# Pooling edges of two blocks as one product over gathered rows, another order in the mixer, and one side of a unit made at once

## The chip, the cores and the metric

The kernel runs on one core of a Trainium2 chip. A core has five engines that run side by side and wait for each other by semaphores: TensorE (PE, matrix products; PEld is its loading of the stationary operand), VectorE (DVE), ScalarE (ACT), GpSimd (POOL) and SyncE (SP), which here only issues transfers. Sixteen DMA engines move the data. The metric is the time of one execution on the device in microseconds (us).

## The reference

One sequence of 512 tokens with 1024 channels passes two layers, all in float32. Layer 0 mixes tokens by pooling, layer 1 by attention over a sliding window; behind each stands a feed-forward network (FFN). What matters here is layer 0's mixer and the first product of both FFNs:

```python
POOL_WINDOWS = (2, 4, 8, 16)          # one for each group of 256 channels
h = rms_norm(x, mix_pre_g[layer])
# per group: mean over the last w tokens (fewer at the start) minus the token itself
mean = (csum[:, 1:, sl] - csum[:, lo, sl]) / cnt[None, :, None]
diffs.append(mean - hf[..., sl])
m = einsum('bsgc,gcd->bsgd', d, w_pool).reshape(B, S, D) * scale
x = x + rms_norm(m, mix_post_g[layer])
u = rms_norm(x, ffn_pre_g[layer]) @ w_in     # 1024 -> 2 * 2816: gate and value
# then a causal convolution of width 3, gelu(gate) * value, and @ w_out
x = x + rms_norm(f, ffn_post_g[layer])
```

## The kernel before

**Blocks.** The tokens stand in four blocks of 128, a block with its tokens on the 128 partitions. The mixer goes through the blocks: the norm of the block (`mix_norm`, lines 379 to 394) leaves `xm`; the pooling (`mix_pool`, 403 to 418) multiplies `xm` with a band matrix and so also transposes it: for each chunk of 128 channels one product makes the block's own 128 output tokens. A window of up to 16 tokens reaches back into the block before, so for blocks 1 to 3 a second product for each chunk (line 416) adds, over the first 16 output tokens, what the previous block's rows give. Eight chunks a block, four to a PSUM bank (`pd`, a bank a half). ScalarE copies both banks to `d`. `mix_map` (420 to 427) multiplies `d` with the group weights `wp`, which VectorE has scaled beforehand (`mix_weights`, 396 to 401) with the channel gains and with `scale_row`, the row of scales spread over the partitions by a product with ones. `mix_post` (a norm, a gain, and the sum into `x`), `mix_pre` (the FFN's norm, `xn_f`) and `mix_T` (eight transposes by PE into `tr_f`) follow; ScalarE copies the transposes to `xTh`, the high part, and VectorE subtracts for `xTl`, the rest.

**Products in two parts.** The large products run as three passes of a faster format: high x high, high x rest, rest x high (`mm3`, 341 to 344). Weights come as `raw` from DRAM by a unit of 1 MB; ScalarE casts them to `wh`, VectorE makes `wl` (`piece`, 205 to 230, by a quarter; `split`, 232 to 262, by a half). `raw` has two buffers, `wh` and `wl` three. A unit of the first FFN product (`up`, 519 to 530) makes 128 gate channels (side 0) and 128 value channels (side 1): for each side eight chunks of the input, three passes each, into a PSUM bank. While not all blocks of `xT` are there, a unit is made for blocks 0 and 1 (256 columns) and later for 2 and 3; the rest of the units run over all 512 columns. The mixed products of the mixer itself are plain float32 and appear as two passes each.

**Order.** The order of PE, ACT, DVE and POOL is the order in which the program issues the instructions (lines 438 to 483 for the mixer, 1128 to 1136 for layer 1); each engine takes its own in that order and waits where an operand isn't ready. SP's transfers are put in order by the framework's scheduler, which holds one back where it isn't ready. SP starts with `x`, the band, constants, the pool weights (unit 0 of the list, `U_POOL`), the rows of gains and the first two units of the FFN (`u0`, `u1`; lines 349 to 362). `u1` takes the `raw` buffer of the pool weights. A block of filler products (`keep_busy`, 366 to 375) runs on PE while the first data come. PSUM has eight banks, all from one ring.

The lines of the mixer's order in the middle, where blocks overlap, are:

```python
    d2 = mix_pool(2)
    piece(u0, 0)
    mix_T(0)
    mix_pre(1)
    piece(u0, 1)
    acc2 = mix_map(2, d2)
```

Of the kernel before, what the change touches and what calls it, by code (L numbers as in the profile page):

```python
# [8 lines left out]
F32 = mybir.dt.float32  # L9
# [51 lines left out]
def _pieces(v, bits, n):  # L61
    out = []
    for _ in range(n - 1):
        q = 2.0 ** (math.floor(math.log2(v)) + 1 - bits)
        c = math.floor(v / q) * q
        out.append(c)
        v -= c
    out.append(float(np.float32(v)))
    return out


def build(nc, tc, ctx, a, out):
# [7 lines left out]
    def bank(name):  # L80
        return ps.tile([P, 512], F32, tag="ps", name=name)
# [193 lines left out]
    def square(junk, src, ss, h, first):  # L275

        nc.scalar.activation(junk, src, AF.Square, scale=1.0 / math.sqrt(D), accum_out=ss[:, h : h + 1])  # L277
        if first:
            nc.gpsimd.tensor_scalar(ss[:, h : h + 1], ss[:, h : h + 1], EPS, None, ALU.add)  # L279

    def new_ss(name):
        return pc.tile([P, 4], F32, tag="ss", name=f"ss_{name}", bufs=6)

    def rstd_end(ss):
        nc.gpsimd.tensor_tensor(ss[:, 2:3], ss[:, 0:1], ss[:, 1:2], ALU.add)
        nc.gpsimd.tensor_tensor(ss[:, 3:4], ss[:, 2:3], mhalf, ALU.pow)
        return ss[:, 3:4]
# [8 lines left out]
    def halves(t):  # L296
        return [t[:, h * 512 : (h + 1) * 512] for h in range(2)]

    def post_norm(b, acc, grow, name, pool=None):
        if pool is None:  # L300
            ts_ = halves(pc.tile([P, D], F32, tag="t4", name=f"pt_{name}{b}", bufs=3))
        else:
            ts_ = [pool.tile([P, 512], F32, tag="qT", name=f"pt_{name}{b}_{h}", bufs=2) for h in range(2)]
        r = rstd_of(acc, ts_, f"p_{name}{b}")
        gs, xs = halves(grow), halves(x[b])
        for h in range(2):
            nc.vector.tensor_tensor(ts_[h], acc[h], gs[h], ALU.mult)
        for h in range(2):
            nc.vector.scalar_tensor_tensor(xs[h], ts_[h], r, xs[h], ALU.mult, ALU.add)
# [45 lines left out]
    nc.sync.dma_start(x[2], a["x"][2])  # L355
    post_row = bcast_row(a["mix_post_g"][0], "mpost0")
    nc.sync.dma_start(x[3], a["x"][3])
    load(U_IN[0])
    pre_row = bcast_row(a["ffn_pre_g"][0], "fpre0")
    load(U_IN[0] + 1)  # L360
    nc.sync.dma_start(cst[:, C_LATE:C_FREQ], a["cst"][:, C_LATE:C_FREQ])
    load_conv(0)
    scale_row = [bank(f"scale_row{h}") for h in range(2)]
    scratch = bank("scratch")

    def keep_busy(n):

        for _ in range(n):
            nc.tensor.matmul(scratch[:, :P], warm, warm, start=True, stop=True)

    keep_busy(13)

    for h in range(2):
        nc.tensor.matmul(scale_row[h], warm, row[:, h * 512 : (h + 1) * 512], start=True, stop=True)
    keep_busy(1)
    wp = pm.tile([P, 8, 256], F32, tag="wp", name="wp")
    xns, xnf = {}, {}

    def mix_norm(b):
        xm = pm.tile([P, D], F32, tag="xm", name=f"xm{b}", bufs=NB)  # L380
        ss = new_ss(f"m{b}")
        xs, junk = halves(x[b]), halves(xm)
        if b < 2:

            nc.scalar.activation(junk[0], xs[0], AF.Square, scale=1.0 / math.sqrt(D), accum_out=ss[:, 0:1])
            nc.vector.tensor_tensor_reduce(out=junk[1], in0=xs[1], in1=xs[1], scale=1.0 / D, scalar=EPS,
                                           op0=ALU.mult, op1=ALU.add, accum_out=ss[:, 1:2])
        else:
            for h in range(2):
                square(junk[h], xs[h], ss, h, h == 0)  # L390
        r = rstd_end(ss)
        for h in range(2):
            nc.vector.tensor_scalar(halves(xm)[h], halves(x[b])[h], r, None, ALU.mult)
        xns[b] = xm

    def mix_weights():
        pr = raws[U_POOL]
        for c in range(8):
            g = c // 2
            nc.vector.scalar_tensor_tensor(wp[:, c, :], pr[:, c * 256 : (c + 1) * 256], gain_col(0, c),  # L400
                                           scale_row[g // 2][:, (g % 2) * 256 : (g % 2 + 1) * 256], ALU.mult, ALU.mult)

    def mix_pool(b):
        d = pm.tile([P, D], F32, tag="d", name=f"d{b}", bufs=2)
        for h in range(2):
            pd = bank(f"pd{b}{h}")
            for k in range(4):
                c = h * 4 + k
                g = c // 2
                cs = slice(c * P, (c + 1) * P)  # L410
                o = pd[:, k * P : (k + 1) * P]
                if b == 0:
                    nc.tensor.matmul(o, xns[b][:, cs], band[:, g, P + EDGE :], start=True, stop=True)
                else:
                    nc.tensor.matmul(o, xns[b][:, cs], band[:, g, :P], start=True, stop=False)
                    nc.tensor.matmul(o[:, :EDGE], xns[b - 1][:, cs], band[:, g, P : P + EDGE], start=False, stop=True)
            nc.scalar.copy(d[:, h * 512 : (h + 1) * 512], pd)
        return d

    def mix_map(b, d):  # L420
        acc = [bank(f"my{b}{h}") for h in range(2)]
        for g in range(4):
            o = acc[g // 2][:, (g % 2) * 256 : (g % 2) * 256 + 256]
            for k in range(2):
                c = g * 2 + k
                nc.tensor.matmul(o, d[:, c * P : (c + 1) * P], wp[:, c, :], start=k == 0, stop=k == 1)  # L426
        return acc

    def mix_post(b, acc):
        post_norm(b, acc, post_row, "m0")  # L430

    def mix_pre(b):
        xnf[b] = pre_norm(b, pre_row, "f0")

    def mix_T(b):
        transpose_in(b, xnf[b], xT, "f0")

    u0, u1 = U_IN[0], U_IN[0] + 1
    mix_norm(0)
    mix_norm(1)  # L440
    d0 = mix_pool(0)
    mix_weights()
    mix_norm(2)
    d1 = mix_pool(1)
    acc0 = mix_map(0, d0)
    mix_post(0, acc0)
    mix_norm(3)
    acc1 = mix_map(1, d1)
    mix_pre(0)
    mix_post(1, acc1)  # L450
    d2 = mix_pool(2)
    piece(u0, 0)
    mix_T(0)
    mix_pre(1)
    piece(u0, 1)
    acc2 = mix_map(2, d2)
    piece(u0, 2)
    mix_post(2, acc2)
    d3 = mix_pool(3)
    mix_T(1)  # L460
    piece(u0, 3)
    mix_pre(2)
    acc3 = mix_map(3, d3)
    piece(u1, 0, defer=True)
    piece(u1, 1, defer=True)
    mix_post(3, acc3)
    while deferred:
        deferred.pop(0)()
    piece(u1, 2)
    piece(u1, 3)  # L470
    mix_pre(3)

    def start0():
        yield 0, (0, 2)
        mix_T(2)
        yield 1, (0, 2), (0,)
        mix_T(3)
        ctx_mix.close()
        yield 1, (0, 2), (1,)
        ahead(U_IN[0])  # L480
        rope_tables()
        yield 0, (2, 4)
        yield 1, (2, 4)


    sin_t = pc.tile([P, NB, 32], F32, tag="sin", name="sin_t")
# [29 lines left out]
        nc.scalar.activation(cos_t, ang, AF.Sin)  # L516


    def up(l, xT, j, accs, blks, sides=(0, 1)):
        hi, lo = slots[U_IN[l] + j]  # L520
        hi4 = hi.rearrange("p (k s c) -> p k s c", k=KC, s=2)
        lo4 = lo.rearrange("p (k s c) -> p k s c", k=KC, s=2)
        if j not in accs:
            accs[j] = [bank(f"u{l}_{j}_{s}") for s in range(2)]
        b0, b1 = blks
        for s in sides:
            o = accs[j][s][:, b0 * P : b1 * P].rearrange("p (b t) -> p b t", t=P)
            for k in range(KC):
                mm3(o, hi4[:, k, s, :], lo4[:, k, s, :],
                    xT[0][:, b0:b1, k, :], xT[1][:, b0:b1, k, :], k == 0, k == KC - 1)  # L530

# [691 lines left out]
```

## Time and profile before

| | |
|---|---|
| median of 3 runs | 910.92 us (910.71 to 912.18) |
| profiled execution | 910.81 us, span 909.0 us |
| PE busy | 900.4 us, 99% of the span |
| VectorE, ScalarE, GpSimd busy | 639.0, 457.9 and 330.0 us |
| DMA | 178.47 MB, 196 GB/s over the span |

The span runs from the first to the last instruction of the profiled execution; what lies around it belongs to its own time. Times in the trace count from the span's start. Matrix products are pipelined, so an instruction's duration on PE is longer than its share of time: the distance from one start to the next is what it costs. A float32 product is one line of the program and two instructions in the trace. The time of a transfer runs from its issue by SP to the landing of its last byte.

### The profile page before, as it was taken

The page shows a single profiled execution, that of the slowest core. Times are in us where ns is not written, and L with a number is a line of the kernel's source. Part 1 is how long each engine was busy: PE and PEld are TensorE (multiplying, and loading weights), DVE is VectorE, ACT ScalarE, POOL GpSimd, SP SyncE. Part 2 cuts the span into 40 slices and gives each one's busy share as a digit, 9 for nine tenths or more (in the row PEclk, how much of TensorE's full clock was granted, in tenths as well). Part 3 has the DMA queues.
Part 4 walks back from the last instruction along what each step waited for, and adds up shares of the span by engine and source line. Part 5 has one row for each costly group of instructions (what it writes and reads, how often), then busy time and mean ns, then how long its engine had stood idle before and what let it go on. Part 6 is the DMA issues. An engine that isn't in the chain of part 4 may idle for free.

```text
span 909.0 us, 12195 instructions
## 1 busy us (share of the span) xinstructions
PE 900.4 (99%) x4416; PEld 762.2 (84%) x4416; DVE 639.0 (70%) x949; ACT 457.9 (50%) x791; POOL 330.0 (36%) x360
## 2 busy tenths in 40 slices
PE   9999999999999999999999999999999999999996
PEld 8998888888888888888888889988888888888885
DVE  5987676676678679855988746655555555777897
ACT  5654444444444566545888635333333333455672
POOL 3418444444441003234655213544444444410031
PEclk9999999999999999999999999999999999999999
DMA  8257887888885666751211252555555555556562
GB/s 315 89 191 267 310 302 262 305 300 289 275 292 156 185 220 231 265 178 45 75 66 47 94 218 95 185 188 203 199 198 195 187 191 189 173 160 191 195 218 109
DMA packets 50207, 178.47 MB, mean 196 GB/s; under 512 B 5473, under 2 KB 13153, under 8 KB 42210
## 3 DMA queue, kind: packets, MB, share of 16 engines
q1 hardware_dynamic: 48272, 164.83, 52.3%
q10 hardware_dynamic: 1874, 12.85, 3.7%
q8 instruction: 35, 0.57, 0.3%
q14 instruction: 26, 0.21, 0.1%
HBM read 139.91 MB, written 37.75 MB: 195 GB/s over the span
## 4 chain that ended last, share of the span: by engine, by line
PE 96%; DVE 1%; DMA 1%; POOL 1%; ACT 0%; issue 0%; ACTq 0%; POOLq 0%; DVEq 0%
PE u L343 18%; PE u L342 18%; PE u L344 18%; PE dn L342 7%; PE dn L343 7%; PE dn L344 7%; PE op L342 2%; PE op L344 2%; PE op L343 2%; PE qp L343 2%; PE my L426 2%; PE qp L344 2%; PE qp L342 1%; PE pT L972 1%; DMA wl<-lo 1%; PE s L937 1%
## 5 line engine op out<-in xcount | busy, mean ns | idle before, releaser
L342 PE MATMUL u<-xTh_f,wh 128*128 128x512 f32 (+1 forms) x768 | 285.7, 372 | 0.0
L343 PE MATMUL u<-xTl_f,wh 128*128 128x512 f32 (+1 forms) x768 | 285.2, 371 | 0.0
L344 PE MATMUL u<-xTh_f,wl 128*128 128x512 f32 (+1 forms) x768 | 285.2, 371 | 0.0
L257 DVE TENSOR_TENSOR wl<-raw,wh 128x1024 fp32r<-128x1024 f32 (+1 forms) x158 | 206.6, 1338 | 33.0 <-ACT wh L256 32.6
L561 ACT ACTIVATE t<-u,conv 128x512 f32<-128x512 f32 x88 | 68.4, 780 | 250.3 <-PE u L344 219.4
L256 ACT CAST wh<-raw 128x1024 fp32r<-128x1024 f32 (+1 forms) x158 | 158.9, 1042 | 56.2 <-DMA raw<-t 41.4
L563 DVE SCALAR_TENSOR_TENSOR t<-u,conv,t 128x511 f32<-128x511 f32 x88 | 65.8, 747 | 147.7 <-ACT t L561 147.7
L342 PEld LDWEIGHTS u<-xTh_f,wh 128*128 128x128 f32 x768 | 144.6, 188 | 25.2
L344 PEld LDWEIGHTS u<-xTh_f,wl 128*128 128x128 f32 x768 | 144.6, 188 | 24.9
L343 PEld LDWEIGHTS u<-xTl_f,wh 128*128 128x128 f32 x768 | 144.6, 188 | 24.8
L582 POOL TENSOR_TENSOR G<-G,G 128x256 f32<-128x256 f32 x22 | 34.4, 1564 | 261.5 <-DVE G L577 261.5
L342 PE MATMUL dn<-wh,gh 128*128 128x512 f32 x276 | 107.6, 390 | 0.0
L344 PE MATMUL dn<-wh,gl 128*128 128x512 f32 x276 | 107.4, 389 | 0.0
L343 PE MATMUL dn<-wl,gh 128*128 128x512 f32 x276 | 107.4, 389 | 0.0
L279 POOL TENSOR_SCALAR ss_p_f<-ss_p_f 128x1 f32<-128x1 f32 x8 | 16.9, 2111 | 158.1 <-ACT dn L277 158.1
L564 DVE SCALAR_TENSOR_TENSOR t<-u,conv,t 128x510 f32<-128x510 f32 x88 | 65.9, 749 | 3.1
L344 PEld LDWEIGHTS dn<-wh,gl 128*128 128x128 f32 x276 | 51.8, 188 | 10.9
L342 PEld LDWEIGHTS dn<-wh,gh 128*128 128x128 f32 x276 | 51.8, 188 | 10.7
L343 PEld LDWEIGHTS dn<-wl,gh 128*128 128x128 f32 x276 | 51.8, 188 | 10.6
L948 ACT ACTIVATE P<-P,stat 128x256 f32<-128x256 f32 (+1 forms) x64 | 30.3, 476 | 11.4 <-DVE stat L945 11.3
L577 DVE TENSOR_TENSOR G<-t 128x512 f32<-128x512 f32 x44 | 32.3, 733 | 5.4 <-ACT t L571 1.0
L591 POOL TENSOR_TENSOR q<-q,q 128x512 f32<-128x512 f32 x22 | 33.0, 1502 | 4.3 <-PE tr_f L335 4.3
(193 smaller groups left out, 1380.6 us busy)
## 6 DMA issues: line engine op xcount, KB each, us to landing
raw<-in_ws_dram SPq DMA_DIRECT2D x46, 1024.0 KB, 5.0
q<-in_ws_dram SPq DMA_DIRECT2D x44, 512.0 KB, 6.1
raw<-t SPq DMA_DIRECT2D x24, 768.0 KB, 5.7
raw<-in_ws_dram SPq DMA_DIRECT2D x28, 512.0 KB, 4.8
t<-q SPq DMA_DIRECT2D x44, 256.0 KB, 2.8
t<-q SPq DMA_DIRECT2D x22, 512.0 KB, 2.8
hi<-h SPq DMA_DIRECT2D x12, 512.0 KB, 6.7
lo<-r SPq DMA_DIRECT2D x12, 512.0 KB, 5.9
```

What stands on the lines that cost most here:

```text
L256: nc.scalar.copy(hi[:, s], r[:, s])
L257: nc.vector.tensor_tensor(lo[:, s], r[:, s], hi[:, s].bitcast(F32), ALU.subtract)
L342: nc.tensor.matmul(acc, ah, bh, start=first, stop=False)
L343: nc.tensor.matmul(acc, ah, bl, start=False, stop=False)
L344: nc.tensor.matmul(acc, al, bh, start=False, stop=last)
L561: nc.scalar.activation(t, u, AF.Identity, bias=conv_col(l, ch, 3), scale=conv_col(l, ch, 2))
L563: nc.vector.scalar_tensor_tensor(t[:, 1:], u[:, : S - 1], conv_col(l, ch, 1), t[:, 1:], ALU.mult, ALU.add)
L564: nc.vector.scalar_tensor_tensor(t[:, 2:], u[:, : S - 2], conv_col(l, ch, 0), t[:, 2:], ALU.mult, ALU.add)
L577: nc.vector.tensor_tensor(g, tg, tv, ALU.mult)
L582: nc.gpsimd.tensor_tensor(s1, s1, G2[:, p, 2, :], ALU.add)
L591: nc.gpsimd.tensor_tensor(b22, b22, b12, ALU.subtract)
L948: nc.scalar.activation(Pt[:, h, 0:w], Pt[:, h, 0:w], AF.Exp, bias=nm[:, h : h + 1], scale=-1.0, accum_out=dn[:, h : h + 1])
```

## The change

In layer 0 the edges of blocks 2 and 3 are made from gathered rows. After the norm of blocks 1 and 2 (step `xe`), eight transfers from SBUF to SBUF collect the block's last 16 rows into a tile `xe`, the 16 rows of chunk c on partitions 16c to 16c + 15. A tile `edge`, zero but for the edge weights of each chunk on the same partitions, is filled once at the start by eight transfers that stand between the load of `x[3]` and that of the first FFN unit. One product for each half then adds the edges of four chunks at once, over 4 x 16 columns. Block 1 keeps its eight edge products.

The functions of the mixer are cut into small steps (`sqa`, `rt`, `xm`, `pd`, `d`, `map`, `psq`, ...), most of them for a half of a block, and the order in which they are issued is written as a list, `MIXER`. The first two FFN units of layer 0 are steps `U` of that list, each of two chunks, one side and two blocks; the casts of their weights are `wh` and `wl`. One filler product goes. Names end in their indices: `pd21` is block 2, half 1; `U1013` is unit 1, blocks 0 and 1, side 1, chunks 6 and 7.

In layer 1 the first two units keep their order up to the value side (side 1) of the second, which is made at the end in one go over all 512 columns; the second unit's gate side for blocks 0 and 1 is cut into two halves of four chunks, with block 3's transposes between them.

```diff
+MIXER = """
+    sqa0 sqa1 srow0 sqb0 rt0 xm00 xm01 sqb1 pd00 srow1 rt1 xm10 d00 xm11 pd01 wp3 d01 xe1 sqa2 wp2 pd10 wp5 sqb2
+    wp1 pd11 wp0 d10 wp7 wp4 sqa3 wp6 map00 eps2 psq00 rt2 xm20 xm21 eps3 peps0 ptt00 map01 xe2 psq01 map10 prt0
+    d11 wh00 ptt01 pd20 pst00 sqb3 map11 psq10 rt3 pst01 wl00 d20 nsq00 nsq01 psq11 pd21 wh10 xm31 xm30 wh01
+    map20 ptt10 d21 wh11 peps1 pd30 neps0 ptt11 nrt0 prt1 nst01 wh02 T01 psq20 nst00 pst10 T00 pd31 pst11 peps2
+    wl01 nsq10 neps1 wl10 map21 nsq11 d30 ptt20 th01 nrt1 tl01 map30 nst10 nst11 d31 T10 th00 wh12 psq21 T11
+    tl00 ptt21 th10 psq30 prt2 tl10 pst20 map31 wh03 th11 ptt30 U1010 nsq20 U0000 psq31 pst21 peps3 wl11 nsq21
...
+"""
...
     nc.sync.dma_start(x[3], a["x"][3])
+    edge = pm.tile([P, KC, EDGE], F32, tag="edge", name="edge")
+    nc.gpsimd.memset(edge, 0.0)
+    for c in range(KC):
+        nc.sync.dma_start(edge[c * EDGE : (c + 1) * EDGE, c, :], a["band"][P - EDGE :, c // 2, P : P + EDGE])
     load(U_IN[0])
...
-    keep_busy(1)
...
+    def xe(b):
+        xes[b] = pm.tile([P, P], F32, tag="xe", name=f"xe{b}", bufs=2)
+        for c in range(KC):
+            nc.sync.dma_start(xes[b][c * EDGE : (c + 1) * EDGE, :], xns[b][P - EDGE :, c * P : (c + 1) * P])
...
+    def pdb(b, h):
+        pd = pds[b, h] = bank(f"pd{b}{h}")
+        for k in range(4):
+            c = h * 4 + k
+            g, cs, o = c // 2, slice(c * P, (c + 1) * P), pd[:, k * P : (k + 1) * P]
+            if b == 0:
+                nc.tensor.matmul(o, xns[b][:, cs], band[:, g, P + EDGE :], start=True, stop=True)
+            else:
+                nc.tensor.matmul(o, xns[b][:, cs], band[:, g, :P], start=k == 0 or b - 1 not in xes, stop=False)
+                if b - 1 not in xes:
                     nc.tensor.matmul(o[:, :EDGE], xns[b - 1][:, cs], band[:, g, P : P + EDGE], start=False, stop=True)
+        if b and b - 1 in xes:
+            nc.tensor.matmul(pd.rearrange("p (k t) -> p k t", k=4)[:, :, :EDGE], xes[b - 1], edge[:, h * 4 : h * 4 + 4, :],
+                             start=False, stop=True)
...
+    def U(u, p, s, q):
+        if (u, p, s, q) == (0, 1, 0, 0):
+            ctx_mix.close()
+            ahead(u0)
+            rope_tables()
+        up(0, xT, u, accs, (2 * p, 2 * p + 2), (s,), range(2 * q, 2 * q + 2))
...
-    accs = ffn_start(0, xT, start0())
+    for step in MIXER.split():
+        name = step.rstrip("0123456789")
+        do[name](*map(int, step[len(name) :]))
...
     def start1():
         yield 0, (0, 2)
         transpose_in(2, xnf[2], xT, "f1")
-        yield 1, (0, 2), (0,)
+        yield 1, (0, 2), (0,), range(0, 4)
         transpose_in(3, xnf[3], xT, "f1")
-        yield 1, (0, 2), (1,)
+        yield 1, (0, 2), (0,), range(4, KC)
         ahead(U_IN[1])
         yield 0, (2, 4)
-        yield 1, (2, 4)
+        yield 1, (2, 4), (0,)
+        yield 1, (0, NB), (1,)
```

## Rows read from the trace of the kernel before

**Rows 1.** Windows: length, then busy us of PE, PEld, DVE, ACT, POOL; PEclk, DMA share, GB/s.
```profile
20.00:40.00 20.00, 20.00 (x147) 19.10 (x146) 17.44 (x29) 15.63 (x41) 9.91 (x20) 1.00 0.22 85
```

**Rows 2.** Waits of PE in the whole span: total us, times, longest us.
```profile
PE scratch L369 <- DVE warm L85: 1.0, 1, 1.0
```

**Rows 3.** Timeline of PE in the mixer: start us, us, instruction, idle before.
```profile
1.04 5.51 PE L369 MATMUL scratch<-warm 128*128 128x128 f32 x26 [1.04 <-DVE warm L85]
6.38 1.88 PE L374 MATMUL scale_row<-row,warm 128*128 128x512 f32 x4
...
8.32 1.95 PE L413 MATMUL pd<-band,xm 128*128 128x128 f32 x16
10.11 0.39 PE L415 MATMUL pd<-band,xm 128*128 128x128 f32 x2
...
13.60 7.15 PE L426 MATMUL my<-wp,d 128*128 128x256 f32 x32
20.59 0.38 PE L415 MATMUL pd<-band,xm 128*128 128x128 f32 x2
```

**Rows 4.** Timeline of PE, layer 1's first product: ten steps apart at 256 and 512 columns.
```profile
561.51 0.28 PE L342 MATMUL u<-xTh_f,wh 128*128 128x256 f32 x1
...
562.70 0.28 PE L343 MATMUL u<-xTl_f,wh 128*128 128x256 f32 x1
...
658.19 0.39 PE L342 MATMUL u<-xTh_f,wh 128*128 128x512 f32 x1
...
660.46 0.39 PE L343 MATMUL u<-xTl_f,wh 128*128 128x512 f32 x1
```

**Rows 5.** Timeline of VectorE, layer 1: the norm of block 3.
```profile
560.54 1.41 DVE L327 SCALAR_TENSOR_TENSOR xn_f<-x,ss_n_f,fpre 128x512 f32<-128x512 f32 x2 [1.78 <-POOL ss_n_f L286]
```

**Rows 6.** Timeline of SP's queue, the first 14 us: start of the issue, its us.
```profile
4.04 1.09 SPq L172 DMA_DIRECT2D raw<-in_ws_dram  x2
...
5.67 0.45 SPq L271 DMA_DIRECT2D mpost<-in_mix_post_g_dram  x1
...
6.90 0.53 SPq L172 DMA_DIRECT2D raw<-in_ws_dram  x1
...
8.67 0.48 SPq L361 DMA_DIRECT2D cst<-in_cst_dram  x1
10.54 0.33 SPq L111 DMA_DIRECT2D conv<-in_cst_dram  x1
13.91 0.33 SPq L172 DMA_DIRECT2D raw<-in_ws_dram  x1
```

**Rows 7.** Transfers up to 80 us: count, KB each, median us to landing.
```profile
raw<-in_ws_dram SPq DMA_DIRECT2D x6, 1024.0 KB, 4.8
raw<-in_ws_dram SPq DMA_DIRECT2D x1, 512.0 KB, 6.5
mpost<-in_mix_post_g_dram SPq DMA_DIRECT2D x1, 512.0 KB, 8.9
raw<-in_ws_dram SPq DMA_DIRECT2D x1, 1024.0 KB, 12.2
cst<-in_cst_dram SPq DMA_DIRECT2D x1, 128.0 KB, 12.1
conv<-in_cst_dram SPq DMA_DIRECT2D x1, 88.0 KB, 10.4
freq<-in_cst_dram SPq DMA_DIRECT2D x1, 16.0 KB, 2.2
```

**Rows 8.** Waits of SP's queue up to 62 us: total us, times, longest us.
```profile
SPq L111 <- DMA raw<-in_ws_dram: 1.4, 1, 1.4
```

**Rows 9.** Timeline of VectorE, the mixer: `xm` of block 1.
```profile
8.61 0.88 DVE L393 TENSOR_SCALAR xm<-x,ss_m 128x512 f32<-128x512 f32 x2 [1.01 <-POOL ss_m L286]
```

**Rows 10.** Windows at the end of the span (columns as in rows 1).
```profile
900.00:905.00 5.00, 1.79 (x8) 1.13 (x7) 4.20 (x7) 1.45 (x4) 1.90 (x4) 1.00 0.18 69
905.00:909.00 4.00, 0.00 (x0) 0.00 (x0) 1.06 (x2) 0.00 (x0) 0.00 (x0) 0.76 0.47 176
```

More of the change, by code (lines that the diff above doesn't have):

```diff
@@ L69, in _pieces @@
     return out
+MIXER = """
[5 more added lines that the diff above has]
+    tl00 ptt21 th10 psq30 prt2 tl10 pst20 map31 wh03 th11 ptt30 U1010 nsq20 U0000 psq31 pst21 peps3 wl11 nsq21
+    wl02 ptt31 U0010 tl11 neps2 U1000 prt3 pst30 pst31 wl03 U0001 U0011 nrt2 wh13 U1011 U1001 U0012 nsq30 U0002
+    nst20 nsq31 U0013 U0003 neps3 wl12 nrt3 T20 nst21 nst31 T21 nst30 th20 U1012 tl20 T30 wl13 th21 U1002 T31
+    th30 th31 tl30 U1003 tl31 U0110 U1100 tl21 U0111 U1013 U1110 U0112 U0100 U1101 U0101 U0113 U0102 U1111 U0103
+    U1102 U1112 U1113 U1103
+"""
 def build(nc, tc, ctx, a, out):
@@ L362, in build @@
     load_conv(0)
-    scale_row = [bank(f"scale_row{h}") for h in range(2)]
     scratch = bank("scratch")
@@ L371, in build @@
     keep_busy(13)
-    for h in range(2):
-        nc.tensor.matmul(scale_row[h], warm, row[:, h * 512 : (h + 1) * 512], start=True, stop=True)
-    keep_busy(1)
[L376 to L382, printed above, removed]
+    wp = pm.tile([P, 8, 256], F32, tag="wp", name="wp")
+    xns, xes, xnf, dts, pds, accm, pts, sss, trs, scale_row = ({} for _ in range(10))
@@ new lines, in build, with srow, square_half @@
+    accs = {}
+    u0 = U_IN[0]
+    def srow(h):
+        scale_row[h] = bank(f"scale_row{h}")
+        nc.tensor.matmul(scale_row[h], warm, row[:, h * 512 : (h + 1) * 512], start=True, stop=True)
+    def square_half(name, b, h, new, src):
+        if h == 0:
+            pts[name, b] = new()
+            sss[name, b] = new_ss(f"{name}{b}")
+        nc.scalar.activation(halves(pts[name, b])[h], src, AF.Square, scale=1.0 / math.sqrt(D),
+                             accum_out=sss[name, b][:, h : h + 1])
@@ L383, in mix_norm, with add_eps, new_xm, sqa @@
+    def add_eps(name, b):
+        ss = sss[name, b]
+        nc.gpsimd.tensor_scalar(ss[:, 0:1], ss[:, 0:1], EPS, None, ALU.add)
+    def new_xm(b):
+        xns[b] = pm.tile([P, D], F32, tag="xm", name=f"xm{b}", bufs=NB)
+        return xns[b]
+    def sqa(b):
+        square_half("m", b, 0, lambda: new_xm(b), halves(x[b])[0])
+    def sqb(b):
         if b < 2:
-            nc.scalar.activation(junk[0], xs[0], AF.Square, scale=1.0 / math.sqrt(D), accum_out=ss[:, 0:1])
-            nc.vector.tensor_tensor_reduce(out=junk[1], in0=xs[1], in1=xs[1], scale=1.0 / D, scalar=EPS,
-                                           op0=ALU.mult, op1=ALU.add, accum_out=ss[:, 1:2])
-        else:
-            for h in range(2):
-                square(junk[h], xs[h], ss, h, h == 0)
@@ L391, in mix_norm @@
[L391 to L415, printed above, removed]
-                    nc.tensor.matmul(o[:, :EDGE], xns[b - 1][:, cs], band[:, g, P : P + EDGE], start=False, stop=True)
-            nc.scalar.copy(d[:, h * 512 : (h + 1) * 512], pd)
-        return d
@@ L420, in mix_map @@
[L420 to L475, printed above, removed]
-        yield 1, (0, 2), (0,)
-        mix_T(3)
-        ctx_mix.close()
-        yield 1, (0, 2), (1,)
-        ahead(U_IN[0])
-        rope_tables()
-        yield 0, (2, 4)
-        yield 1, (2, 4)
+            x1 = halves(x[b])[1]
@@ new lines, in sqb, with xm @@
+            nc.vector.tensor_tensor_reduce(out=halves(xns[b])[1], in0=x1, in1=x1, scale=1.0 / D, scalar=EPS,
+                                           op0=ALU.mult, op1=ALU.add, accum_out=sss["m", b][:, 1:2])
+        else:
+            square_half("m", b, 1, None, halves(x[b])[1])
+    def xm(b, h):
+        nc.vector.tensor_scalar(halves(xns[b])[h], halves(x[b])[h], sss["m", b][:, 3:4], None, ALU.mult)
+    def xe(b):
+        xes[b] = pm.tile([P, P], F32, tag="xe", name=f"xe{b}", bufs=2)
+        for c in range(KC):
+            nc.sync.dma_start(xes[b][c * EDGE : (c + 1) * EDGE, :], xns[b][P - EDGE :, c * P : (c + 1) * P])
@@ new lines, in wps @@
+    def wps(c):
+        g = c // 2
+        nc.vector.scalar_tensor_tensor(wp[:, c, :], raws[U_POOL][:, c * 256 : (c + 1) * 256], gain_col(0, c),
+                                       scale_row[g // 2][:, (g % 2) * 256 : (g % 2 + 1) * 256], ALU.mult, ALU.mult)
+    def pdb(b, h):
[8 more added lines that the diff above has]
+                if b - 1 not in xes:
+                    nc.tensor.matmul(o[:, :EDGE], xns[b - 1][:, cs], band[:, g, P : P + EDGE], start=False, stop=True)
+        if b and b - 1 in xes:
+            nc.tensor.matmul(pd.rearrange("p (k t) -> p k t", k=4)[:, :, :EDGE], xes[b - 1], edge[:, h * 4 : h * 4 + 4, :],
+                             start=False, stop=True)
@@ new lines, in db, with mapb, new_t4 @@
+    def db(b, h):
+        if h == 0:
+            dts[b] = pm.tile([P, D], F32, tag="d", name=f"d{b}", bufs=2)
+        nc.scalar.copy(halves(dts[b])[h], pds[b, h])
+    def mapb(b, h):
+        acc = accm[b, h] = bank(f"my{b}{h}")
+        for c in range(4 * h, 4 * h + 4):
+            g, k = divmod(c, 2)
+            o = acc[:, (g % 2) * 256 : (g % 2) * 256 + 256]
+            nc.tensor.matmul(o, dts[b][:, c * P : (c + 1) * P], wp[:, c, :], start=k == 0, stop=k == 1)
+    def new_t4(name):
+        return lambda: pc.tile([P, D], F32, tag="t4", name=name, bufs=3)
@@ new lines, in psq, with ptt, pst, nsq @@
+    def psq(b, h):
+        square_half("p", b, h, new_t4(f"pt_m{b}"), accm[b, h])
+    def ptt(b, h):
+        nc.vector.tensor_tensor(halves(pts["p", b])[h], accm[b, h], halves(post_row)[h], ALU.mult)
+    def pst(b, h):
+        xs = halves(x[b])[h]
+        nc.vector.scalar_tensor_tensor(xs, halves(pts["p", b])[h], sss["p", b][:, 3:4], xs, ALU.mult, ALU.add)
+    def nsq(b, h):
+        square_half("n", b, h, new_t4(f"xn_f{b}"), halves(x[b])[h])
+    def nst(b, h):
+        nc.vector.scalar_tensor_tensor(halves(pts["n", b])[h], halves(x[b])[h], sss["n", b][:, 3:4], halves(pre_row)[h],
+                                       ALU.mult, ALU.mult)
@@ new lines, in T, with of_xT, th, tl @@
+    def T(b, h):
+        pt = trs[b, h] = bank(f"tr_f{b}{h}")
+        for k in range(4):
+            kc = h * 4 + k
+            nc.tensor.transpose(pt[:, k * P : (k + 1) * P], pts["n", b][:, kc * P : (kc + 1) * P], ident)
+    def of_xT(i, b, h):
+        return xT[i][:, b, h * 4 : (h + 1) * 4, :].rearrange("p k t -> p (k t)")
+    def th(b, h):
+        nc.scalar.copy(of_xT(0, b, h), trs[b, h])
+    def tl(b, h):
+        nc.vector.tensor_tensor(of_xT(1, b, h), trs[b, h], of_xT(0, b, h).bitcast(F32), ALU.subtract)
@@ new lines, in build, with wh @@
+    lows = {}
+    def wh(u, q):
+        piece(u0 + u, q, defer=True)
+        lows[u, q] = deferred.pop()
+    def U(u, p, s, q):
[4 more added lines that the diff above has]
+        up(0, xT, u, accs, (2 * p, 2 * p + 2), (s,), range(2 * q, 2 * q + 2))
+    do = {"srow": srow, "sqa": sqa, "sqb": sqb, "eps": lambda b: add_eps("m", b), "rt": lambda b: rstd_end(sss["m", b]),
+          "xm": xm, "xe": xe, "wp": wps, "pd": pdb, "d": db, "map": mapb, "psq": psq, "peps": lambda b: add_eps("p", b),
+          "prt": lambda b: rstd_end(sss["p", b]), "ptt": ptt, "pst": pst, "nsq": nsq,
+          "neps": lambda b: add_eps("n", b), "nrt": lambda b: rstd_end(sss["n", b]), "nst": nst, "T": T, "th": th,
+          "tl": tl, "wh": wh, "wl": lambda u, q: lows.pop((u, q))(), "U": U}
@@ L516, in rope_tables, with up @@
         nc.scalar.activation(cos_t, ang, AF.Sin)
-    def up(l, xT, j, accs, blks, sides=(0, 1)):
+    def up(l, xT, j, accs, blks, sides=(0, 1), ks=range(KC)):
         hi, lo = slots[U_IN[l] + j]
@@ L522, in up @@
         lo4 = lo.rearrange("p (k s c) -> p k s c", k=KC, s=2)
-        if j not in accs:
-            accs[j] = [bank(f"u{l}_{j}_{s}") for s in range(2)]
         b0, b1 = blks
         for s in sides:
+            if s not in accs.setdefault(j, {}):
+                accs[j][s] = bank(f"u{l}_{j}_{s}")
             o = accs[j][s][:, b0 * P : b1 * P].rearrange("p (b t) -> p b t", t=P)
-            for k in range(KC):
+            for k in ks:
                 mm3(o, hi4[:, k, s, :], lo4[:, k, s, :],
@@ L1130, in start1 @@
         transpose_in(2, xnf[2], xT, "f1")
-        yield 1, (0, 2), (0,)
+        yield 1, (0, 2), (0,), range(0, 4)
         transpose_in(3, xnf[3], xT, "f1")
-        yield 1, (0, 2), (1,)
+        yield 1, (0, 2), (0,), range(4, KC)
         ahead(U_IN[1])
         yield 0, (2, 4)
-        yield 1, (2, 4)
+        yield 1, (2, 4), (0,)
+        yield 1, (0, NB), (1,)
     post_row = bcast_row(a["ffn_post_g"][1], "fpost1")
```

## The prediction

> **What bounds the kernel now.** I read the mixer's stretch of the windows first: TensorE (PE) is busy for all of the 20 us from 20 to 40, VectorE for 17.4, ScalarE for 15.6 [rows 1]. The waits say how strictly: PE's longest wait of the whole span is 1.0 us for its first operand [rows 2]. So the kernel gets shorter only by PE work that goes away, and any new wait of PE adds its full length. Then PE's order of time through the mixer, for the prices [rows 3]. Last the transfers: a PE with no gap says that data came in time, not by how much, and the change puts 24 more transfers into SP's queue in the first 30 us.
>
> **PE work removed.** Block 0 pools without an edge: 16 passes from 8.32 to 10.11, 0.112 us each. Block 1 takes from 10.11 to 13.60, 3.49 us, so its eight edge products (16 passes over 16 columns) cost 3.49 - 1.79 = 1.70 us, 0.106 a pass [rows 3]; blocks 2 and 3 repeat the pattern. After the change these two have one edge product for each half, two passes each over 64 columns: four passes a block. No row has 64 columns in this form. The neighbours are 0.106 at 16 columns and 0.112 at 128, so 0.42 to 0.45; I take 0.43. Saved: 2 x (1.70 - 0.43) = 2.5 us (3.4 if they cost nothing).
>
> The Trainium skill ("TensorE: Matmul & The Clock Gate", section "Back-to-back issue gap") puts a small matmul at a floor of about 62 ns where the sequencer decodes it; four passes would by that be 0.25 us a block, an estimate, and the saving 2.9.
>
> The lone filler product ahead of block 0 goes, two passes or 0.22 us. In layer 1, 48 products over 256 columns become 24 over 512. Ten steps take 1.19 us at 256 columns and 2.27 at 512 [rows 4], so that saves 24 x (2 x 0.119 - 0.227) = 0.26 us. Block 3's transposes there now follow 12 products and not 24: they would start nine steps after 561.51, at 562.6, and their input is done at 561.95 [rows 5]. So I cost this move at nothing, 0.6 us being the cover; if the norm were a microsecond late it would cost 0.4. In layer 0 the first two units keep 192 products over 256 columns, and one more switch from transposes to products costs some 0.1. VectorE's, ScalarE's and GpSimd's work in sum hardly changes; where a gap opens on PE, they gain on it. **Sum without a wait: -2.9 us, 907.9.**
>
> **The transfers.** Issue times stand in [rows 6], times from issue to landing in [rows 7]. Two things in them decide. First, SP goes through eight completion semaphores in turn, so a transfer waits until the one eight places ahead has landed. The conv constants need nothing, yet issue at 10.54 after 1.4 us of waiting for a transfer of raw [rows 8]; that is the first half of the pool weights, issued at 4.04 and landed 6.5 later, at 10.54, and with the row that the ACT queue sends it is number 8 where conv is number 16. Second, a transfer lands behind what was issued ahead of it: the late constants, 128 KB, took 12.1 us from 8.67 and conv 10.4, where alone 16 KB took 2.2.
>
> The eight edge transfers are numbers 13 to 20, right behind x3. They go out only as numbers 5 to 12 land, among them the pool weights at 10.5, the post gains at 14.6 (5.67 + 8.9) and x3 at about 16.1 (unit 0's weights, 6.90 + 12.2, land at 19.1; x3's 512 KB are the first third of what lies between). So the last edge leaves at 16.1, and unit 0's weights, queued behind it, at 16.5 where they left at 6.90. With nothing left ahead they take the 4.8 us of the usual megabyte: 21.3. The pre gains, the late constants and conv follow and land at about 22.8, 23.2 and 23.4, at that rate of 3 us a megabyte.
>
> The gathers of block 1's last rows (xe1) may be read from 9.49, when xm1 is done [rows 9]. As numbers 25 to 32 four find their semaphores free (edges) and four wait for unit 0, the gains, the constants and conv. The last leaves at 23.5 and lands 2.2 later: **25.7**.
>
> PE needs them early. Its order is the two rows of scales and blocks 0 and 1, then map 00, 01 and 10, then pooling 20. Block 1 ends 0.2 earlier than before, 13.4; three map halves of 1.75 ((20.59 - 13.60)/4) make 18.6; pooling 20's own eight passes 0.9: at **19.5** PE stands at the edge product, and all of its other work is queued behind. It waits 25.7 - 19.5 = 6.2 us. ScalarE meanwhile holds at the first cut of unit 0 until 21.3, which this wait covers. The second set, xe2, goes out behind unit 1's load (left 23.9, landed 28.7) and is in by about 31.0; PE gets there after 0.2 + 1.75 + 1.1 + 1.75 + 0.9 us, at 31.4: covered, by 0.4.
>
> An idle PE also loses its clock. At the end PE's last work stops at 901.8 and the mean granted clock from 905 to 909 is 0.76 [rows 10], so it fell from full to half (2.4 to 1.2 GHz) at 907.1, after 5.3 us of nothing. At the start 26 passes took 5.34 us [rows 3]; at 0.223 and 0.112 each that is 4.9 us at the low level. A gap of 6.2 us would lower it, and 4.9 us of work at half speed costs 2.4. The bounds are 0 (it doesn't fall) and 2.5.
>
> **Sum: +6.2 + 2.4 - 2.9 = +5.7 on the profiled execution's 910.81 us (span 909.0): 916.5.** The median of the runs, 910.92, lies 0.1 above that execution; 916.5 stands for both.
>
> **Rivals.** (1) Unit 1's load goes out ahead of the gathers: its buffer is free at 13.9, and SP's order isn't written by hand. Then 1 MB more, 3.0 us, lies before them: landing 28.7, wait 9.2, sum +8.7: 919.5. For it: SP put that load behind the constants only while it wasn't ready [rows 6].
>
> (2) The wait is as forecast but the clock stays; or SP places the gathers ahead of unit 0, and the gap splits into a short wait at pooling 20 and others at map 20 (its input stands on ScalarE behind unit 0's cut) and pooling 30, 6.3 together: +6.3 - 2.9, 914.2.
>
> (3) The other side: the gathers are in before 19.5. Readable at 9.5, eight issues at the 0.33 of conv's, landed in 2.2, they would be in at 14.4 if neither the semaphores nor the backlog held them, and the whole -2.9 shows: 907.9. It decides at the landing of the eighth gather. The 12.1 and 10.4 us of transfers that left at the same moments speak against it. The Trainium skill ("DMA: Bandwidth & Descriptors", section "Anatomy of one DMA — SWDGE (gpsimd) path") gives a DMA 2.0 us plus its bytes at 436 GB/s, fitted on GpSimd's path; for eight gathers of 8 KB that would be this case. The trace has 10.4 us for 88 KB on SP's.
>
> (4) Only the backlog counts, not the semaphores: the gathers land like conv, at 20.9 and a little, 21.4; wait 1.9, no loss of clock: 909.8.
>
> **How the numbers follow.** The forecast has 0.38, with its own range 914.5 to 918.5; rival 1 0.20; rival 2 0.20; rival 3 0.14; rival 4 0.08. About 0.2%, 1.8 us, is what a measurement of this kernel tells from no change: slower is 0.38 + 0.20 + 0.20 = 0.78, same 0.08, faster 0.14. The doubt is nearly all of one thing: where SP's order puts 24 small transfers and what each waits for. The range goes from rival 4 to just over rival 1, 909.5 to 920.5, and leaves out rival 3 and a longer wait.
>
> **What would show it.** Right: the edge product of pd on PE idle 5 to 9 us, some 20 us into the span, released by a transfer into xe; raw of unit 0 issued after 15 us; a granted clock under 1.00 in the stretch after; the passes over 16 columns down from 48 to 16; PE without gaps after 40 us. Wrong: no gap at that product, or the eighth gather landing before 19.5. A wait at a transpose would put the fault in the order of ScalarE and VectorE instead, and a wait at 562 into layer 1's move.

## The result and the profile after

The changed kernel took 918.74 us (median of 6 runs, 918.22 to 919.12) against 910.86 us for the kernel before beside it (6 runs, 910.45 to 912.18): a ratio of 1.0084 with a 95% interval of 1.0071 to 1.0097. It is slower by 7.9 us. The profiled execution took 918.87 us, span 917.1.

What answers to the rows of before comes first from PE. Its waits in the whole span (total us, times, longest us) have a new first line beside the one of [rows 2]:

```profile
PE pd L454 <- DMA xe<-xm: 9.0, 1, 9.0
```

PE's timeline of the mixer (start us, us, instruction, idle before) shows where it stands; L450 is now the pooling product of a block, L454 the edge product over gathered rows, L467 the map:

```profile
18.73 1.05 PE L450 MATMUL pd<-band,xm 128*128 128x128 f32 x8
28.75 0.66 PE L454 MATMUL pd<-edge,xe 128*128 128x64 f32 x2 [8.96 <-DMA xe<-xm]
29.20 3.41 PE L467 MATMUL my<-wp,d 128*128 128x256 f32 x8
32.45 1.05 PE L450 MATMUL pd<-band,xm 128*128 128x128 f32 x8
33.34 0.33 PE L454 MATMUL pd<-edge,xe 128*128 128x64 f32 x2
33.51 1.95 PE L467 MATMUL my<-wp,d 128*128 128x256 f32 x8
35.29 1.05 PE L450 MATMUL pd<-band,xm 128*128 128x128 f32 x8
36.18 0.33 PE L454 MATMUL pd<-edge,xe 128*128 128x64 f32 x2
```

There is one hole, from 19.8 to 28.75, at the first edge product of block 2. The eight map products behind it take 3.41 us, the same eight at 33.51 only 1.95. The windows (length, busy us of PE, PEld, DVE, ACT, POOL, then PEclk, DMA share, GB/s) say why; the first answers to [rows 1]:

```profile
20.00:40.00 20.00, 11.25 (x64) 10.31 (x65) 8.50 (x15) 10.64 (x28) 5.37 (x12) 0.74 0.32 114
...
21.00:22.00 1.00, 0.00 (x0) 0.00 (x0) 0.00 (x0) 0.43 (x1) 0.00 (x0) 0.96 1.03 274
22.00:23.00 1.00, 0.00 (x0) 0.00 (x0) 0.69 (x1) 1.00 (x4) 0.11 (x1) 0.50 0.90 251
...
32.00:33.00 1.00, 1.00 (x8) 0.95 (x7) 0.00 (x0) 0.35 (x1) 0.29 (x1) 0.92 0.07 14
```

The granted clock falls to half (from 2.4 to 1.2 GHz) near 21.9 and comes back near 32.1.

SP's queue, which answers to [rows 6] (start of the issue, its us; several issues of one line stand together):

```profile
7.26 8.85 SPq L378 DMA_DIRECT2D edge<-in_band_dram  x8
16.15 0.92 SPq L187 DMA_DIRECT2D raw<-in_ws_dram  x1
...
18.11 0.69 SPq L187 DMA_DIRECT2D raw<-in_ws_dram  x1
18.84 0.45 SPq L126 DMA_DIRECT2D conv<-in_cst_dram  x1
19.34 13.23 SPq L435 DMA_DIRECT2D xe<-xm  x16
```

The eight edge transfers, 1 KB each, hold the queue for 8.85 us. Unit 0's weights leave at 16.15 where they left at 6.90 [rows 6], and unit 1's (the second line with raw) leave at 18.11, ahead of all gathers. SP's own waits up to 40 us say what stood between, to be read beside [rows 8]:

```profile
SPq L378 <- DMA raw<-in_ws_dram: 3.0, 2, 2.0
SPq L378 <- DMA x<-in_x_dram: 2.1, 3, 0.9
SPq L435 <- DMA raw<-in_ws_dram: 2.0, 2, 1.7
SPq L435 <- DMA fpre<-in_ffn_pre_g_dram: 1.4, 1, 1.4
SPq L378 <- DMA mpost<-in_mix_post_g_dram: 1.0, 1, 1.0
```

None of these transfers is an input of the one that waits: an edge load needs nothing of the pool weights, a gather nothing of the pre gains. What each waits for is the transfer eight places ahead in SP's own list, whose completion semaphore it uses again (the eight are called the ring below, one of them a slot). The chain of waits that leads to PE's hole (stretch 10 to 35 us; start us, us, what) closes the account:

```profile
18.11 8.24 DMA raw<-in_ws_dram
...
26.37 0.51 SPq L435
...
26.92 1.73 DMA xe<-xm
```

Unit 1's megabyte lands at 26.35, only then do the last two gathers of block 2 go out, and the last lands at 28.65. Of SP's issues unit 1's load is the 23rd and the gather that leaves at 26.37 the 31st. The slot is the smaller part of this, though: the sixth gather left at 24.09, without waiting for that load, and took 3.6 us, so it too landed behind the megabyte, at 27.7. What the slot adds to the backlog at this point is the last 1.0 us. From there on the kernel runs as before, later: unit 2's first product over 512 columns, before and after, starts at

```profile
61.06 0.40 PE L342 MATMUL u<-xTh_f,wh 128*128 128x512 f32 x1
```

```profile
69.17 0.40 PE L357 MATMUL u<-xTh_f,wh 128*128 128x512 f32 x1
```

so all 8.1 us of the two profiles' difference are there by then; what follows takes 847.9 us in both (909.0 − 61.06 and 917.1 − 69.17).

### The profile page after: what moved, and what is told of

Same layout as the page of the kernel before. It is cut to its first block, busy times and chain, and to the rows that moved or that the text cites. A ratio compares the mean times of both kernels' runs of the same rounds, so it can differ in the third digit from the quotient of the medians.

```text
span 917.1 us, 12134 instructions
## 1 busy us (share of the span) xinstructions
PE 899.2 (98%) x4366; PEld 758.9 (83%) x4366; DVE 639.8 (70%) x949; ACT 458.2 (50%) x791; POOL 330.4 (36%) x361
## 4 chain that ended last, share of the span: by engine, by line
PE 91%; DVE 3%; DMA 2%; issue 1%; ACT 1%; POOL 1%; SPq 0%; DVEq 0%; POOLq 0%; ACTq 0%
PE u L359 18%; PE u L358 17%; PE u L357 17%; PE dn L359 6%; PE dn L358 6%; PE dn L357 6%; DMA raw<-in_ws_dram 2%; PE op L357 2%; PE op L359 2%; PE qp L357 2%; PE qp L359 2%; PE op L358 2%; PE qp L358 2%; PE my L467 2%; PE pT L1012 1%
## 5 line engine op out<-in xcount | busy, mean ns | idle before, releaser
L294 POOL TENSOR_SCALAR ss_p_f<-ss_p_f 128x1 f32<-128x1 f32 x8 | 19.7, 2463 | 156.0 <-ACT dn L292 156.0
```

## The experiments

Theory A: the loss is PE's wait for block 2's gathered rows and the clock that goes with it, and the wait comes from SP's completion order and backlog; PE's work itself became about 2.9 us shorter. Rivals: B, the new order of the mixer costs; C, unit 1's place in SP's queue is of no account; D, only the backlog counts, and slots of the ring do no harm; E, the backlog lies in the DMA engines, so that another queue helps little. "Before" beside these runs measured 911.5 to 911.6 us.

### Order alone

```diff
-    edge = pm.tile([P, KC, EDGE], F32, tag="edge", name="edge")
-    nc.gpsimd.memset(edge, 0.0)
-    for c in range(KC):
-        nc.sync.dma_start(edge[c * EDGE : (c + 1) * EDGE, c, :], a["band"][...])
...
     def xe(b):
+        return
```

> The changed kernel without its gathers: no transfers into edge and xe, blocks 2 and 3 make their edges with eight products each as before; the list's order, the missing filler and layer 1's part stay. Theory A (PE waits for the gathered rows, because SP's eight completion semaphores and the backlog delay them): no wait at pooling 20, and only the filler and layer 1 are saved, 910.8 - 0.2 - 0.3 + 0.1 = 910.4. Rival B (the new order of ScalarE and VectorE is what costs): most of the +7.9 stays, 916 or more.

Measured: 911.48 us, ratio 0.9998 (0.9989 to 1.0008). No wait of PE in the mixer; unit 2's first product at 61.34. The order costs nothing that can be measured, so B falls. The 0.4 us expected of the filler and of layer 1 lies within the interval (1.0 under to 0.7 over), so this run can't tell it.

### Rows there at once

```diff
-    for c in range(KC):
-        nc.sync.dma_start(edge[c * EDGE : (c + 1) * EDGE, c, :], a["band"][...])
...
         xes[b] = pm.tile([P, P], F32, tag="xe", name=f"xe{b}", bufs=2)
-        for c in range(KC):
-            nc.sync.dma_start(xes[b][c * EDGE : (c + 1) * EDGE, :], xns[b][...])
+        nc.gpsimd.memset(xes[b], 0.0)
```

(both tiles then hold zeros, so the edges of blocks 2 and 3 are left out)

> The changed kernel with edge and xe set by GpSimd and not by transfers; it leaves out the edges of blocks 2 and 3 (they are zero), all products and the order stay. It shows what the change would give if the rows came in time. Theory A: no wait of PE over 0.5 us in the mixer, 907.9, the forecast's sum without a wait. Rival B: 914 or more.

Measured: 908.38 us, ratio 0.9963 (0.9950 to 0.9976), 3.1 us under the kernel before. With the products kept and only the 24 transfers gone, the whole sum of PE's work shows, and the difference to the change, about 11 us, is the transfers'.

### Unit 1 behind the gathers

```diff
-    load(U_IN[0] + 1)
     nc.sync.dma_start(cst[:, C_LATE:C_FREQ], a["cst"][:, C_LATE:C_FREQ])
...
+        if b == 1:
+            load(U_IN[0] + 1)
```

(the second part at the end of `xe`)

> The changed kernel with the load of unit 1's weights issued behind the first eight gathers. Theory A, with the forecast's own case: the last gather then waits for the landing of conv at about 24.0 instead of unit 1's at 26.4 and lands near 26.2; PE waits about 6.5 us instead of 9.0, and with 1.7 for the clock the time is about 916. Rival C (the wait is set by the 24 small transfers themselves, not by what stands among them): still 9 us and 918.7.

Measured: 916.28 us, ratio 1.0054 (1.0038 to 1.0071). PE's timeline, SP's issues, and two windows of the clock:

```profile
25.78 0.66 PE L455 MATMUL pd<-edge,xe 128*128 128x64 f32 x2 [5.58 <-DMA xe<-xm]
```

```profile
18.82 5.69 SPq L434 DMA_DIRECT2D xe<-xm  x8
24.61 0.53 SPq L187 DMA_DIRECT2D raw<-in_ws_dram  x1
```

```profile
24.00:26.00 2.00, 0.22 (x1) 0.25 (x2) 1.14 (x3) 0.00 (x0) 0.18 (x1) 0.85 0.41 55
26.00:28.00 2.00, 2.00 (x6) 1.69 (x7) 0.00 (x0) 1.46 (x4) 0.18 (x1) 0.50 0.74 283
```

With that one transfer behind, the wait is 5.6 us instead of 9.0, and the last gather leaves at 23.9 and lands at 25.64, beside the forecast's 23.5 and 25.7. C falls, and the forecast's own case is this kernel: 4.8 us over the kernel before, where the forecast has 5.7. By the ratios 2.7 of the change's loss come back, less than the 3.4 by which the wait is shorter; the profile shown is the fastest of the four runs (915.12 to 916.68).

### The edge weights in one transfer

```diff
-    nc.gpsimd.memset(edge, 0.0)
-    for c in range(KC):
-        nc.sync.dma_start(edge[c * EDGE : (c + 1) * EDGE, c, :], a["band"][...])
+    nc.sync.dma_start(edge.rearrange("p c t -> p (c t)"), a["edge"])
```

(`a["edge"]` holds the same numbers ready-made, 64 KB)

> The changed kernel with the tile edge loaded ready-made from DRAM in one transfer of 64 KB instead of eight. Theory A: unit 0's weights leave at about 7.5 again; the gathers find their semaphores as x2, mpost, x3, edge, unit 0, the gains and conv land, the last one leaves at about 21.7, behind unit 1's megabyte, and lands near 25: PE waits about 5.3 us, time about 915. Rival D (only the backlog ahead of a transfer counts, not the semaphores): the gathers leave from 10 us on and are in by 21.5, wait 1.8, about 910.

Measured: 915.74 us, ratio 1.0047 (1.0032 to 1.0062); PE waits 6.2 us. SP's queue:

```profile
8.39 0.53 SPq L187 DMA_DIRECT2D raw<-in_ws_dram  x1
...
13.90 5.80 SPq L433 DMA_DIRECT2D xe<-xm  x5
20.84 0.34 SPq L187 DMA_DIRECT2D raw<-in_ws_dram  x1
22.02 6.83 SPq L433 DMA_DIRECT2D xe<-xm  x11
```

Unit 0 leaves 7.8 us earlier than in the change, and five gathers go out from 13.9 on; but they are again held one by one, unit 1's load goes out among them, and the last three of block 2 follow behind it. The eight small loads account for some 3.4 us of the change's loss (1.0084 against 1.0047). D (gathers from 10 us on, 1.8 us of wait) does not hold: the gathers leave one by one from 13.9 on, most of them when an older transfer has landed. My own 5.3 us of wait was 0.9 short.

### Gathers issued by GpSimd

```diff
-            nc.sync.dma_start(xes[b][c * EDGE : (c + 1) * EDGE, :], xns[b][...])
+            nc.gpsimd.dma_start(xes[b][c * EDGE : (c + 1) * EDGE, :], xns[b][...])
```

(with the edge weights in one transfer, as above)

> The tile edge in one transfer, and all sixteen gathers issued by GpSimd and not by SP, on its own queue with its own semaphores. Theory A (semaphore slots of SP and the backlog of SP's queue): the rows of block 1 don't wait for SP's transfers any more; if GpSimd issues one in about 1 us they are in by about 19, PE waits under 1 us, and the time is 1 to 3 us under the kernel before. Rival E (the backlog is in the DMA engines, whatever queue a transfer comes by): they land behind what SP sent, at 21 to 22, wait about 2 us, time about 1 us under to 1 us over before.

Measured: 910.62 us, ratio 0.9988 (0.9979 to 0.9997). GpSimd's timeline and PE's waits:

```profile
10.32 4.11 POOL L433 DMA_DIRECT2D xe<-xm  x8 [0.84 <-DVE xm L428]
...
18.58 3.95 POOL L433 DMA_DIRECT2D xe<-xm  x8 [0.29 <-issue]
```

```profile
PE pd L448 <- DVE xm L428: 2.2, 2, 1.4
```

PE's wait for a gather is gone. Away from SP's ring all eight of block 2 go out as soon as the rows are there. The second set, though, keeps GpSimd busy for 3.95 us from 18.58, in front of its steps of block 3's norm, and PE then waits 1.4 us for block 3's `xm` (the other 0.8 is block 1's, at 10 us). Behind that wait the clock falls too:

```profile
28.00:30.00 2.00, 1.81 (x9) 1.84 (x10) 2.00 (x5) 1.31 (x4) 0.60 (x1) 0.50 0.00 0
```

In this profile, the slowest of the ten runs (911.57), all that was saved is used up there; the median keeps 1.0 us of it.

### Gathers through DRAM

```diff
-        for c in range(KC):
-            nc.sync.dma_start(xes[b][c * EDGE : (c + 1) * EDGE, :], xns[b][...])
+        h = pd.tile([P, P], F32, tag=f"xd{b}", name=f"xd{b}")
+        nc.gpsimd.dma_start(h.rearrange("(c t) p -> t c p", c=KC), xns[b][...])
+        (nc.gpsimd if b == 1 else nc.sync).dma_start(xes[b], h)
```

(with the edge weights in one transfer)

> The tile edge in one transfer; the rows go from SBUF to a scratch tile in DRAM in one transfer and from there into xe in one more, both by GpSimd for block 1, the second by SP for block 2: four transfers instead of sixteen. Theory A: from 9.8 two issues of about 1 us and two landings of about 2 us each, in by about 16: no wait at pooling 20, 2 to 3 us under before. Rival E: each of the two stands behind SP's backlog, in after 21: wait 2 to 5 us, time from 1 under to 3 over before.

Measured: 912.85 us, ratio 1.0011 (0.9999 to 1.0023). Times to landing in the first 40 us, and PE's wait:

```profile
xe<-xd POOLq DMA_DIRECT2D x1, 64.0 KB, 6.2
xe<-xd SPq DMA_DIRECT2D x1, 64.0 KB, 1.7
```

```profile
PE pd L453 <- DMA xe<-xd: 2.6, 1, 2.6
```

For block 2 the trip from DRAM, one transfer of 64 KB, takes 6.2 us while SP's megabytes are in flight, after some 5 for the trip into it; the rows are there near 22.8. For block 3, when the megabytes are through, the second trip takes 1.7. The two go by different queues, but SP's own gathers of 8 KB in the next run show the same, 7.9 us for the first and 1.7 for the last. So E holds in part: another queue gets round SP's completion ring, not round the backlog. The ten runs spread from 910.79 to 914.74; those under 911.3 have a mean clock of 0.997 or 0.998, those over 914, the profiled one among them, 0.995. So the wait is not the whole of the loss here either.

### Block 3 alone

```diff
-... wp3 d01 xe1 sqa2 ...
+... wp3 d01 sqa2 ...
...
     load_conv(0)
+    nc.sync.dma_start(edge.rearrange("p c t -> p (c t)"), a["edge"])
```

(the eight edge loads go; block 2 keeps its eight edge products)

> Only block 3's edges come from gathered rows (eight gathers by SP, behind unit 1's load); block 2 makes its own with eight products; the tile edge comes in one transfer behind conv. Theory A: the gathers find their semaphores as mpost to unit 1 land and are in by about 25.5, and PE reaches pooling 30's edge about 26: no wait or a short one, 1.27 + 0.2 + 0.3 - 0.1 = 1.6 us under before. Rival B (order): no gain.

Measured: 909.47 us, ratio 0.9980 (0.9970 to 0.9989): faster than both kernels. SP's last issues and PE at block 3:

```profile
15.40 0.33 SPq L187 DMA_DIRECT2D raw<-in_ws_dram  x1
17.01 8.22 SPq L433 DMA_DIRECT2D xe<-xm  x8
```

```profile
27.52 0.33 PE L452 MATMUL pd<-edge,xe 128*128 128x64 f32 x2
```

The gathers are held as before, the last leaves at 24.7 and lands 1.7 us later, at 26.4; but block 3's edge product stands at 27.5, and PE doesn't wait.

### PE kept busy in the wait

```diff
+        if (b, h) == (2, 0):
+            fill = bank("fill")
+            for _ in range(36):
+                nc.tensor.matmul(fill[:, :P], ident, ident, start=True, stop=True)
         if b and b - 1 in xes:
```

> The changed kernel with 36 filler products (72 passes of 0.112 us, 8.1 us) on PE just ahead of pooling 20's edge product, inside its wait of 9.0 us: only the clock is kept up, the rows come when they came. Theory A: the clock stays at its full level and the 1.7 us that PE loses at half speed after the wait come back: about 917.0 where the changed kernel has 918.7, 6.2 over before. If the clock costs nothing, it stays at 7.9 over.

Measured: 917.18 us, ratio 1.0064 (1.0049 to 1.0079); unit 2's first product at 67.79 instead of 69.17. PE's wait shrinks to 0.7 us and the clock stays at 1.00:

```profile
28.00:32.00 4.00, 3.33 (x23) 2.96 (x22) 0.02 (x1) 2.46 (x8) 0.63 (x3) 1.00 0.06 12
```

The rows arrive no earlier, so what comes back is the clock's: 1.4 us by the profile, 1.8 by the ratios. The intervals of the two ratios meet (1.0071 to 1.0097 for the change), so the size rests on the profile.

### A queue for each block

```diff
-            nc.sync.dma_start(xes[b][c * EDGE : (c + 1) * EDGE, :], xns[b][...])
+            (nc.gpsimd if b == 1 else nc.sync).dma_start(xes[b][c * EDGE : (c + 1) * EDGE, :], xns[b][...])
```

(with the edge weights in one transfer)

> The edge weights come ready-made in one transfer, block 2's eight gathers are issued by GpSimd and block 3's eight by SP. Theory (what costs is the time at which rows land before block 2's pooling, and what GpSimd issues in front of its norm steps later): block 2's rows land by 19.7 us as they did with all sixteen on GpSimd, the second set no longer stands in front of GpSimd's norm steps, PE waits for neither, and unit 2's first product comes near 58.2 us (61.1 less the 2.9 of PE's work saved): ratio 0.9968, some 2.9 us under the kernel before, and 1 us under the version with block 3 alone. Rival (a gather by GpSimd in front of block 2 costs PE's start as well, through GpSimd's first steps): a wait of PE on a product of GpSimd before 24 us, unit 2 later than 60, no gain over block 3 alone (ratio 0.998 or more).

Measured: 909.36 us, ratio 0.9975 (0.9966 to 0.9984). GpSimd's issues, times to landing in the first 40 us, and PE's waits:

```profile
10.58 4.12 POOL L433 DMA_DIRECT2D xe<-xm  x8 [0.83 <-DVE xm L428]
```

```profile
xe<-xm POOLq DMA_DIRECT2D x8, 8.0 KB, 5.7
```

```profile
PE pd L448 <- DVE xm L428: 0.7, 1, 0.7
...
PE pd L452 <- issue: 0.2, 1, 0.2
```

Block 2's rows are in by 19.8, 0.3 us before PE gets to its edge product, which doesn't wait. Unit 2's first product starts at 59.16, where 58.2 was expected. At block 3's edge product PE is idle for 0.2 us; the profile lists that under "issue", but SP's last gather left at 24.28 and landed at 26.00, just before the product's start at 26.09, so it was most likely a wait for that gather. PE also waits 0.7 us at 10.3 for block 1's `xm`, before any gather. The 2.9 of PE's work lie within the interval (1.5 to 3.1 us under the kernel before), so what these two waits cost isn't shown. The interval meets that of block 3 alone, so which of these two is the better stays open; both beat the kernel before.

## Why the prediction was right, and where it was off

**Direction and mechanism.** Right. PE stops once, at the place named (block 2's edge product, reached at 19.8 for a forecast of 19.5), for the reason named, and every microsecond of it reaches the end. 918.74 lies in the range, 2.2 us above the forecast and 0.2 above the range that the forecast's own case was given: 9.0 of wait and 1.7 of clock, less 2.9, is +7.8, and +7.9 was measured. The case that came is rival 1, and its 919.5 is the nearer number. That the forecast is off by no more than 2.2 owes something to luck: the wait was 2.8 longer than forecast, the clock's share 0.7 smaller.

**The term that was mis-sized: the wait, 6.2 forecast, 9.0 measured.** The step that failed is the place of unit 1's load in SP's order. I put it behind the gathers, because before the change it went behind the constants. In the changed kernel it leaves at 18.11, ahead of the conv constants and of all sixteen gathers, so all eight gathers land behind its megabyte. That is rival 1, down to the numbers (landing 28.7, wait 9.2). In the run with that load behind the gathers the wait is 3.4 us shorter. [rows 6] already had the warning: the load left at 13.91 as soon as its buffer was free, so SP's order follows readiness, and 0.20 was too little for that case.

**The edge loads.** Right, nearly to the digit: the last of eight leaves at 15.8 (16.1 forecast), unit 0 at 16.15 (16.5), and ScalarE's first cast of its data starts at 21.57 (forecast for the landing: 21.3). Eight transfers of 1 KB cost SP 8.9 us because six of them wait, 6.1 us together, for the landing of an older, large one. The single transfer in their place shortens the wait by 2.8 us.

**PE's work, −2.9.** Right: −3.1 without the transfers (interval −4.6 to −2.2). The edge product for half a block is cheaper than I took it, 33.34 to 33.51, 0.17 us for two passes, so 0.085 a pass where my 0.43 a block makes 0.11. Two blocks then save 2.7 us (3.49 − 1.79 − 0.34 each), not 2.5. The Trainium skill ("TensorE: Matmul & The Clock Gate", section "Back-to-back issue gap") puts the floor at about 62 ns where the sequencer decodes the product; the trace's 0.085 lies above it.

**Layer 1 and the filler, −0.5 together.** Layer 1's part was right, too small for the times to show but not for the traces: from block 2's transposes in layer 1 to the first product of that layer's unit 2 it is 19.00 us before (560.28 to 579.28) and 18.71 in the change (568.39 to 587.10), 0.29 less for a forecast of 0.26, with no new wait at block 3's transposes. That the whole stretch from layer 0's unit 2 to the end takes 847.9 us in both profiles doesn't contradict it: in the ten profiles with the new layer 1 that stretch runs from 846.9 to 849.7. The filler's 0.22 can't be read off, because the start of single profiles differs by more (see the last section).

**The second set.** Covered, as forecast, but by more: SP's sixteenth gather ends its issue at 32.6 (19.34 + 13.23) after some 0.6, so with the 1.73 us to land that the chain shows it is in near 33.7, and PE gets to block 3's edge product at 36.18. With 9 us of wait ahead of it PE came later than in the forecast.

**The clock, 2.4 forecast, 1.7 measured.** It did fall. The cost is 0.28 at the edge product (0.45 to the next start instead of 0.17) and 1.47 at the map (32.45 − 29.20 for 35.29 − 33.51). I had read the time at half speed from the start of the kernel, 4.9 us of work; here PE worked 3.4 us before the clock was back. One place did not give the number for another.

**The other rivals.** Without the clock's loss (rival 2) the time would be that of the run with filler products, 917.2. Rows in time (rival 3) is what the runs with 908.4, 909.4 and 909.5 us had to be built for. Only the backlog (rival 4) fell with the single edge transfer: the wait stays at 6.2. The Trainium skill's fit ("DMA: Bandwidth & Descriptors", section "Anatomy of one DMA — SWDGE (gpsimd) path") of 2.0 us plus bytes at 436 GB/s, made on GpSimd's path, would make 2.0 us of 8 KB, an estimate; GpSimd's 8 KB took 5.7 here (median of eight). They left while SP's megabytes were in flight, and no run here has them without these, so how much of the 5.7 is the backlog isn't shown. SP's gathers with the backlog gone come near it, with 1.7 us.

## What to carry to other kernels

Before adding small transfers, count the slots: a transfer that waits for the landing of an older one turns a kilobyte into a microsecond, and it holds whatever is queued behind it. Compute for each gather which older, large transfer it will wait for and what will be in flight when it leaves, and take every load that is ready as standing ahead of it. A gather that feeds a saturated engine pays where its consumer comes after the backlog (block 3 here) and costs where it comes before (block 2), unless it has a queue of its own whose engine can spare the issue time.

## What was not expected of the hardware

**The clock's fall.** It came at very different times: in the change 2.1 us after PE's last product, with unit 1 behind the gathers about 5.2 us after (PE idle from 20.2, the clock at 0.85 from 24 to 26), at the end of the kernel before 5.3 [rows 10]. With the gathers by GpSimd it fell at 28.0 though PE's waits just before it were 1.4 and 0.5 us, with products between them. One such number from one place is no constant.

**The start.** The same 26 filler passes took 5.51 us in the profile of before [rows 3], 4.97 in the change's, 5.91 with block 3 alone and 5.01 with a queue for each block. In the change block 1's pooling begins at 9.44, 0.7 us earlier than in [rows 3] where 0.2 was forecast, for this reason as much as for the filler. The clock records of the traces tell what differs. They begin, at the full level, at 5.99 us in the profile of before and at 4.85 in the change's (a window ahead of the first record shows 1.00 without one); up to there the filler passes stand 0.213 us apart, behind it 0.112. Over the eleven profiles this first record lies between 4.1 and 7.2 us. Where the passes end early and block 1's `xm` is later, as with a queue for each block, PE waits for that instead. Positions in single profiles are therefore good to about 1 us here; effects smaller than that need the medians, or two marks in the same profile as for layer 1.

**GpSimd as an issuer.** Eight issues took it 4.1 us, about half a microsecond each, and its norm steps stand behind them. In the run with a queue for each block, where it issues only the first set, PE doesn't wait for block 3's `xm`.
